# Five feed-forward blocks begun on the first token half, kept in memory, and the T3 operands made on VectorE

## The chip, the cores and the metric

The kernel runs on one core of one Trainium2 chip. A core has TensorE for matrix products, VectorE, ScalarE and GpSimd for elementwise work, queues that issue memory transfers (those of SyncE and ScalarE are used here), an on-chip memory (SBUF) and the accumulators of TensorE (PSUM). The metric is the device time of one execution in microseconds. All arithmetic is float32 or the 32-bit format of TensorE's products (fp32r).

## The reference

One layer of a hybrid decoder for 1,024 prompt tokens and 8 sample tokens that share the weights, 1,032 tokens in all, with a model width of 1,024. Three mixers (a gated short convolution, a state-space scan, a cross-attention) read one normalized input, are gated, added and merged; then comes the part that the change touches:

```
def swiglu(xn, w_gate, w_up, w_down):
    return (jax.nn.silu(xn @ w_gate) * (xn @ w_up)) @ w_down
...
xp = xp + h
xp = xp + swiglu(rmsnorm(xp, norm_ffn_w[l]), w_ffn_gate[l], w_ffn_up[l], w_ffn_down[l])
```

The hidden width is 2,816, that is 22 blocks of 128 columns. The same is done for the sample tokens, and a last normalization follows.

## The kernel before

**Layout.** Activations lie transposed: 8 tiles of 128 channels by 1,032 tokens. A float32 product is made of three fp32r products: each operand is split into a high part (a cast on ScalarE) and the rest (a subtraction on VectorE), and TensorE multiplies high by high, high by low and low by high. `st_split` does this for weights (L220), `split_to` for activations (L327).

**Stages.** The three mixers, their gates and the merge take until about 1,864 us of the span; the merge (L1522 to L1555) goes over the tokens in two halves of 516 and leaves the sums of the residual in eight tiles `x2`. Then come the gate and up products of the feed-forward part (L1568 to L1619), and then the down product and the last normalization.

**The fast matrix product.** The gate and up products are made pair by pair: pair (g, j) holds the hidden blocks j and j+1 of `w_ffn_gate`, pair (u, j) those of `w_ffn_up`, for j = 0, 2, ... 20. Weights and activations are cut into two by two blocks: the activations by the first and last four channel tiles and by the two token halves (B11 and B21 are the first token half, B12 and B22 the second), the weights by the same channel halves and the two hidden blocks. `strassen` (L271) makes the four output blocks from seven products in place of eight. Its operands on the activation side are B11, B21, B22 and four sums and differences of blocks, named T1, nT2, T3 and T4 in the code. They are the "forms": for each, four tiles of 128 x 516 are computed, cast (high) and subtracted (low), once for all 22 pairs. On the weight side, S, T and D are built for every pair from the two raw weight blocks (`st_sums`, `st_sums2`). One product (`st_prod`, L230) is 24 matmuls of 128 x 128 by 258 columns: four channel tiles, three fp32r products, two halves of columns. Products accumulate in PSUM tiles `m0`, `m1`, `m2` of two banks each.

**The order of the products.** For a plain pair: weights A times B11, S times T1, S times nT2, A times B21, T times T3, T times B22, D times T4, with evictions to the output tiles between them (ScalarE copies and VectorE adds and subtracts). For the first three pairs, (g, 0), (u, 0) and (g, 2), `st_early` (L242) makes the two products that need B11 and B21 alone, ahead of all the others. Those forms come from the first token half, whose merge and normalization are done earlier (`form_first` and `form_second`, queued in the merge's second half). The result of `st_early`, a tile of 128 x 1,032, holds A times B11 in its second half and the finished output block of the first token half in its first. It stays in a slot of the pool `ev`, and `strassen` takes it as `early` and makes only the other five products; it then reaches the second half of that tile through `S.copy(o21, o12)` (L307), `V.tensor_sub` (L308) and `V.tensor_tensor` (L309).

**The forms of the second token half.** After the last merge block, the norm of the second half is made (`norm_half`), and the forms follow in the order T1, nT2, T3, B22, T4 (L1571 to L1591), with the sums of g0's weights among them (`g0`). All are made by VectorE with ScalarE's casts, but for T3: its difference and its low part are GpSimd's (L1583, L1584).

**Slots.** The pool `ev` has 5 slots: early tiles, weight sums, `sq` and `rf` of the norm. Raw weights have 3 slots (`raw`), split weights 3 each (`whi`, `wlo`). The pool `big` has 8, which hold the eight `x2` tiles until the forms are made and the outputs of the pairs after that.

**What sets the order.** The order of instructions on each engine is fixed when the program is built: a planner goes through the program with modelled durations, and places an instruction when its inputs and slots are there by that model. Three chains keep weight loads, casts and splits in program order (`in_turn`, L110). Weight loads, reloads and the stores of the hidden blocks are issued by SyncE's queue; the stores of `x2` by ScalarE's.

Of the kernel before, what the change touches and what calls it, by code (L numbers as in the profile page):

```python
# [12 lines left out]
ALU = mybir.AluOpType  # L13
# [4 lines left out]
P = 128  # L18
# [3 lines left out]
TT = T + NS  # L22
# [19 lines left out]
def tile_kernel(ctx: ExitStack, tc, a, o):  # L42
    nc = tc.nc
    V, S, G, PE, SY = nc.vector, nc.scalar, nc.gpsimd, nc.tensor, nc.sync

    def f32(t):
        return t.bitcast(F32)
# [13 lines left out]
    def mm_ps(name):  # L61
        return pmm[0].tile([P, NCH, 512], F32, tag="mm", name=name)

    def sm_ps(name):
        return psm.tile([P, 512], F32, tag="sm", name=name)

    def dram(name, shape):
        return dp.tile(shape, F32, tag=name, name=name)

    def act_tile(part, name, dt=F32R, shape=(P, TT)):  # L70
        return ap_.tile(list(shape), dt, tag=part, name=name)
# [4 lines left out]
    def t3(t, lo=0):  # L76
# [9 lines left out]
        out=tri, in_=ones, pattern=[[1, P]], compare_op=ALU.is_ge, fill=0.0,  # L86
# [23 lines left out]
    def in_turn(key, ins):  # L110
        if key in prev:
            tc.add_manual_dep(
                ins.ins, prev[key].name,
                mybir.DependencyInfo(mybir.DependencyClass.NoSync, mybir.DependencyReason.DATA),
                reason="in_turn",
            )
        prev[key] = ins.ins
# [28 lines left out]
    def weights(src, name):  # L146
        raw = loaded.pop(name, None)
        if raw is None:
            raw = load_raw(src, name)
        hi = wp.tile([P, 1024], F32R, tag="whi", name=name + "h")  # L150
        lo = wp.tile([P, 1024], F32R, tag="wlo", name=name + "l")
        in_turn("hi", S.copy(hi, raw))
        in_turn("lo", V.tensor_sub(lo, raw, f32(hi)))
        return hi, lo

    def ev_tile(name, shape=(P, TT + 4), dt=F32):
        return ev.tile(list(shape), dt, tag="ev", name=name)
# [22 lines left out]
    def gemm(w, acts, name, width=P, off=0):  # L180

        hi, lo = w
        ps = mm_ps(name)
        nk = len(acts)
        marks = {nk * i // pace[0] for i in range(pace[0])}
        for k, (ah, al) in enumerate(acts):
            if k in marks:
                tick()
            ks = slice(k * width + off, k * width + off + P)
            for i, (wt, x) in enumerate(((hi, ah), (hi, al), (lo, ah))):  # L190
                for n in range(NCH):
                    PE.matmul(  # L192
                        ps[:, n, :CW], wt[:, ks], x[:, n * CW : (n + 1) * CW],
                        start=(k == 0 and i == 0), stop=(k == nk - 1 and i == 2),
                    )
        return ps

    def wblock(w, col):
        return w[:, col : col + P].rearrange("(k p) c -> p k c", p=P)
# [5 lines left out]
    HS = [slice(0, HT), slice(HT, TT)]  # L205
# [3 lines left out]
    def h3(t):  # L209
        return t.rearrange("p (n c) -> p n c", n=2)  # L210

    def hv(ps):
        return ps[:, :2, :HC]

    def st_raw(src, name):
        raw = wp.tile([P, 1024], F32, tag="raw", name=name)
        in_turn("raw", SY.dma_start(raw.rearrange("p (k c) -> p k c", k=KD), src))
        return raw

    def st_split(src, name, n=1024):  # L220
        hi = wp.tile([P, 1024], F32R, tag="whi", name=name + "h")
        lo = wp.tile([P, 1024], F32R, tag="wlo", name=name + "l")
        in_turn("hi", S.copy(hi[:, :n], src))
        in_turn("lo", V.tensor_sub(lo[:, :n], src, f32(hi)[:, :n]))
        return hi, lo

    def st_ps(tag, name):
        return pst[0].tile([P, 2, 512], F32, tag=tag, name=name)

    def st_prod(forms, ps, w, off, f, start):  # L230
        for kt in range(4):
            xh, xl = forms[f][kt]
            ks = slice(off + kt * P, off + (kt + 1) * P)
            for i, (wt, x) in enumerate(((w[0], xh), (w[0], xl), (w[1], xh))):
                for n in range(2):
                    PE.matmul(  # L236
                        ps[:, n, :HC], wt[:, ks], x[:, n * HC : (n + 1) * HC],
                        start=(start and kt == 0 and i == 0), stop=(kt == 3 and i == 2),
                        skip_group_check=True,
                    )  # L240

    def st_early(blocks, forms):  # L242


        held = []
        for i, (src1, nm, o1) in enumerate(blocks):
            wA = st_split(st_raw(src1, f"{nm}Er"), f"{nm}E")
            ps = st_ps(f"m{i}", f"{nm}e")
            st_prod(forms, ps, wA, 0, "B11", True)
            S.copy(h3(o1[:, HS[1]]), hv(ps))  # L250
            held.append((wA, ps, o1))
        for wA, ps, o1 in held:
            st_prod(forms, ps, wA, 512, "B21", False)
            S.copy(h3(o1[:, HS[0]]), hv(ps))

    def st_sums(src1, src2, nm, sums):
        raw1, raw2 = st_raw(src1, f"{nm}r1"), st_raw(src2, f"{nm}r2")
# [5 lines left out]
    def st_sums2(raw1, raw2, sa, nm, sums):  # L263
        sb = sums(f"{nm}sb")
        V.tensor_add(sb[:, :512], raw1[:, :512], raw2[:, :512])
        V.scalar_tensor_tensor(
            sb[:, 512:], sa[:, 512:], -1.0, raw1[:, 512:], op0=ALU.mult, op1=ALU.subtract
        )
        return st_split(sb, f"{nm}T")
# [54 lines left out]
            return o21  # L324
        return hv(pa)

    def split_to(hi, lo, src, eng=V):  # L327
        S.copy(hi, src)
        eng.tensor_tensor(lo, src, f32(hi), op=ALU.subtract)


    xT_d = dram("xT_d", [KD, P, TT])
# [7 lines left out]
    r_d = dram("r_d", [1, TT])  # L340
    x2_d = dram("x2_d", [KD, P, TT])
    h_d = dram("h_d", [NF, P, TT])
    q_d = dram("q_d", [8, P, TT])
    k_d = dram("k_d", [2, P, D])
    v_d = dram("v_d", [2, P, D])
# [23 lines left out]
    with tc.tile_pool(name="p0", bufs=1) as p0:  # L369
# [13 lines left out]
        for key, src, n in (  # L383
# [14 lines left out]
            while done < n:  # L398
                b, off = divmod(at, P)
                m = min(n - done, P - off)  # L400
# [3 lines left out]
        ps = sm_ps("ps_prm")  # L404
# [26 lines left out]
        for g3 in range(3):  # L431
# [3 lines left out]
            src = [(t, P) for t in xin[3 * g3 : 3 * g3 + 3]]  # L435
# [3 lines left out]
            for i, (t, n) in enumerate(src):  # L439
                j = 3 * g3 + i  # L440
# [10 lines left out]
            ps = sm_ps(f"ps_rb{g3}")  # L451
            blocks(ps, lambda i, t, n: bc(rst[:n, 3 * g3 + i : 3 * g3 + i + 1], [n, P]))
            V.tensor_copy(rbc[:, c], ps[:, :n_all])
            for k in range(KD):
                ps = sm_ps(f"ps_xt{g3}{k}")
# [13 lines left out]
    for src, dst, nr, nt in (  # L469
# [4 lines left out]
        for q0 in range(0, nt, per):  # L474
            t = ev_tile(f"hist{nr}_{q0}", (nr, per * P))
            SY.dma_start(t, src[:, q0 * P : (q0 + per) * P])
            ps = sm_ps(f"ps_h{nr}_{q0}")
# [23 lines left out]
    def small(name):  # L501
        return pd_.tile([P, W], F32, tag=name, name=name)

    x0, mx, u, z, z2, q = (small(n) for n in ("x0", "mx", "u", "z", "z2", "q"))
# [948 lines left out]
    def big(name):  # L1453
        return ph2.tile([P, TT], F32, tag="big", bufs=8, name=name)
# [3 lines left out]
    for m in range(KD):  # L1458
# [4 lines left out]
        ps = gemm(weights(wblock(a["w_attn_o"][0], m * P), f"wo3{m}"), acts, f"po3{m}")  # L1463
# [36 lines left out]
    def normed(m, half):  # L1500
        t = x2[m][:, HS[half]]
        V.scalar_tensor_tensor(t, t, par("ffn", m), rfs[half][:, :HT], op0=ALU.mult, op1=ALU.mult)  # L1502
        return t


    forms = {}
    fx = {}

    def form(f, kt, src, eng=V):
        if kt % 2 == 0:  # L1510
            mk = fx.get(f) or (lambda part, nm: act_tile(part, nm, shape=(P, 2, HT)))
            pair = (mk("ah", f"{f}{kt}h"), mk("al", f"{f}{kt}l"))
            forms.setdefault(f, []).extend(tuple(t[:, i, :] for t in pair) for i in range(2))
        split_to(*forms[f][kt], src, eng)

    def form_first(kt):
        form("B11", kt, normed(kt, 0))
# [4 lines left out]
    for half in range(2):  # L1522
        sq = ev_tile(f"sq{half}")
        for m in range(KD):
# [3 lines left out]
            ps = mm_ps(f"pm{half}{m}")  # L1528
# [12 lines left out]
            t = x2[m][:, HS[half]]  # L1541
# [24 lines left out]


    ffn = {"g": a["w_ffn_gate"][0], "u": a["w_ffn_up"][0]}  # L1568
    early = {(nm, j): ev_tile(f"{nm}{j}e") for nm, j in (("g", 0), ("u", 0), ("g", 2))}
    st_early([(wblock(ffn[nm], j * P), f"{nm}{j}", t[:, :TT]) for (nm, j), t in early.items()], forms)  # L1570
    for kt in range(4):  # L1571
        b12, b11 = normed(kt, 1), x2[kt][:, HS[0]]
        V.tensor_sub(b11, b12, b11)
# [3 lines left out]
    for kt in range(4):  # L1577
        t1, b22 = x2[kt][:, HS[0]], normed(kt + 4, 1)
        V.tensor_sub(t1, t1, b22)
        form("nT2", kt, t1)  # L1580
    for kt in range(4):
        b12, b22 = x2[kt][:, HS[1]], x2[kt + 4][:, HS[1]]
        G.tensor_tensor(b12, b22, b12, op=ALU.subtract)  # L1583
        form("T3", kt, b12, G)  # L1584
    g0 = (*g0, st_sums2(*g0[:3], "g0", ev_sums))
    for kt in range(4):
        form("B22", kt, x2[kt + 4][:, HS[1]])
# [5 lines left out]
    def hidden_pair(nm, j):  # L1593
        o = []
        e = early.get((nm, j))

        def outs():
            o.extend([big(f"{nm}{j}o1") if e is None else e[:, :TT], big(f"{nm}{j}o2")])
            return tuple(t[:, c] for t in o for c in HS)

        src = ffn[nm]
        pa = strassen(
            wblock(src, j * P), wblock(src, (j + 1) * P), forms, f"{nm}{j}",
            ev_sums, outs, e, ready=g0 if (nm, j) == ("g", 0) else None,
        )
        return o[0], o[1], pa if e is None else h3(pa)
# [99 lines left out]
    for n3 in range(3):  # L1706
        c0, c1 = 384 * n3, min(384 * n3 + 384, TT)
        w = c1 - c0
        for m0 in range(0, KD, 3):
            ms = range(m0, min(m0 + 3, KD))  # L1710
            ps = mm_ps(f"pl{n3}{m0}")
# [46 lines left out]
```

## Time and profile before

| what | value |
|---|---|
| median of 3 runs | 2605.4 us (2601.82 to 2606.6) |
| the profiled execution | 2603.75 us, span 2601.7 us |
| mean granted clock of TensorE | 0.988 |
| TensorE busy | 2521.7 us, 97% of the span |
| VectorE busy | 1466.5 us, 56% |
| ScalarE busy | 936.6 us, 36% |
| GpSimd busy | 197.9 us, 8% |
| memory traffic | 389.31 MB, mean 150 GB/s |

A row of a timeline has the start and the length of a group of like instructions in microseconds, the engine (PE is TensorE, PEld its weight loads, DVE is VectorE, ACT ScalarE, POOL GpSimd, SP SyncE; a q behind the name is the engine's queue), the line of the kernel, the operation, the tile written and those read, their shapes and the count; a bracket tells the idle time before and what ended it. Many instructions of the feed-forward part have the line of a helper (L236 for the matmuls of `st_prod`, L329 for the low parts of the forms, L224 for those of the weights), so they are told apart by their tiles: `g0m` is the PSUM of pair (g, 0), `g0e` that of its early block, `T10l` the low part of form T1. A row of stages has, for each engine, busy time and count, then the granted clock, the share of the DMA engines and GB/s.

### The profile page before, as it was taken

To read this page: it belongs to the slowest core of one execution; us is meant where nothing else is said; L and a number is where in the kernel's file an instruction comes from. 1 tells how busy PE (TensorE), PEld (TensorE's weight loads), DVE (VectorE), ACT (ScalarE), POOL (GpSimd) and SP (SyncE) were. 2 spreads that over 40 slices of the span, in tenths; PEclk is the share of its full clock that TensorE was granted. 3 is DMA by queue.
4 is the path that set the end of the run, shared out by engine and by line. 5 is a ranking of instruction groups with operands and counts; after the bars stand their busy time and mean duration, and the time that the engine had idled before them with its cause. 6 is when DMAs were issued, how large, how long until landed. Compare 5 with 4: busy or idle time off the path is not lost.

```text
span 2601.7 us, 42760 instructions
## 1 busy us (share of the span) xinstructions
PE 2521.7 (97%) x18037; PEld 2453.8 (94%) x18037; DVE 1466.5 (56%) x2037; ACT 936.6 (36%) x1434; POOL 197.9 (8%) x211
## 2 busy tenths in 40 slices
PE   7999999999998999999999999999989999999998
PEld 5899999999998999999999898999979999999998
DVE  5844586866667655555566633444784445454316
ACT  6643444553232235354342322213343333341202
POOL 0000000013213123023000000000010000000000
PEclk9999999999999999999999999999989999999999
DMA  6244333376556755665487757854322222265211
GB/s 190 94 138 156 124 104 106 123 206 148 154 157 138 161 185 160 176 196 150 133 292 243 273 175 252 299 173 144 122 73 82 74 90 66 82 212 163 66 41 66
DMA packets 391422, 389.31 MB, mean 150 GB/s; under 512 B 15622, under 2 KB 337782, under 8 KB 391223
## 3 DMA queue, kind: packets, MB, share of 16 engines
q1 hardware_dynamic: 372654, 335.74, 43.4%
q10 hardware_dynamic: 18577, 50.84, 5.1%
q8 instruction: 142, 2.33, 0.4%
q14 instruction: 49, 0.40, 0.0%
HBM read 280.41 MB, written 106.34 MB: 149 GB/s over the span
## 4 chain that ended last, share of the span: by engine, by line
PE 68%; DMA 5%; DVE 4%; issue 1%; ACT 1%; SPq 0%; POOL 0%; ACTq 0%; DVEq 0%; POOLq 0%
PE ps_g L192 10%; PE po L192 10%; PE pd L192 8%; PE ps_scc L192 4%; PE pm L1535 4%; PE ps_q L192 4%; PE ps_scx L192 3%; PE ps_scb L192 3%; DMA kc<-in_cache_mem_k_dram 1%; PE py L797 1%; PE pss L815 1%; PE po L789 1%; DMA r<-ac_d 1%; PE u20m L236 1%; PE g20m L236 1%
## 5 line engine op out<-in xcount | busy, mean ns | idle before, releaser
L1658 DVE TENSOR_TENSOR x<-pd,x 128x1032 f32<-128x1032 f32 x24 | 29.5, 1231 | 131.4 <-PE pd L192 131.4
L742 ACT ACTIVATE r<-r,acum 128x128 f32<-128x128 f32 x256 | 78.9, 391 | 36.2 <-DMA r<-ac_d 34.8
L1424 DVE TENSOR_TENSOR gt<-po,gt 128x1032 f32<-128x1032 f32 x24 | 29.5, 1230 | 70.4 <-PE po L192 69.1
L776 POOL TENSOR_TENSOR xdd<-xdt,decst 128x512 f32<-128x512 f32 x32 | 46.6, 1456 | 268.1 <-DVE xdt L772 268.1
L1583 POOL TENSOR_TENSOR x<-x,x 128x516 f32<-128x516 f32 x4 | 8.9, 2235 | 635.8 <-DVE x L1502 635.8
L598 DVE SCALAR_TENSOR_TENSOR ax<-u,prm,ax 128x1024 f32<-128x1024 f32 x44 | 56.4, 1281 | 0.3 <-ACT ax L595 0.3
L882 POOL TENSOR_TENSOR st<-st,xb 128x512 f32<-128x512 f32 x32 | 43.8, 1368 | 36.2 <-DVE xb L876 34.0
L769 ACT COPY bT<-bp 128x128 f32<-128x128 f32 x32 | 8.5, 264 | 105.4 <-DVE cbm L767 105.4
L770 DVE TENSOR_TENSOR r<-r,cbm 128x1024 f32<-128x1024 f32 x32 | 39.1, 1222 | 8.6 <-ACT r L743 8.0
L806 DVE SCALAR_TENSOR_TENSOR x<-x,dpar,yt 128x128 f32<-128x128 f32 x128 | 37.5, 354 | 10.1 <-ACT yt L804 9.2
L828 POOL TENSOR_TENSOR s<-s,cdec 128x512 f32<-128x512 f32 x28 | 39.1, 1398 | 46.1 <-DVE s L821 29.6
L821 DVE TENSOR_TENSOR s<-pss,s 128x512 f32<-128x512 f32 x28 | 19.3, 688 | 38.8 <-PE pss L815 38.8
L815 PE MATMUL pss<-xdd,bT 128*128 128x512 f32 x64 | 33.8, 610 | 6.6 <-ACT bT L769 6.5
L879 POOL TENSOR_TENSOR st<-st,es 128x512 f32<-128x512 f32 x32 | 36.6, 1143 | 20.3 <-DMA st<-in_state_ssm_dram 16.7
L797 PE MATMUL py<-r,xdt 128*64 128x128 f32 x512 | 35.0, 279 | 1.5 <-issue 1.5
L767 DVE TENSOR_TENSOR cbm<-bp,tri 128x128 f32<-128x128 f32 x32 | 9.3, 290 | 45.3 <-PE bp L762 45.2
L743 ACT ACTIVATE r<-r 128x1024 f32<-128x1024 f32 x32 | 33.9, 1059 | 0.7
L793 DVE TENSOR_TENSOR yt<-po,ea 128x512 f32<-128x512 f32 x28 | 19.2, 686 | 25.7 <-PE po L789 25.7
L797 PEld LDWEIGHTS py<-r,xdt 128*64 128x64 f32 x512 | 27.3, 136 | 5.8 <-issue 2.4
L1263 ACT ACTIVATE pr<-psa,mx 128x256 f32<-128x256 f32 x32 | 14.9, 472 | 48.8 <-DVE mx L1261 48.8
L1253 DVE TENSOR_TENSOR kc<-kc,qb 128x1024 f32<-128x1024 f32 x16 | 19.6, 1224 | 22.0 <-DMA kc<-in_cache_mem_k_dram 21.9
L1542 DVE TENSOR_TENSOR x<-pm,xT 128x516 f32<-128x516 f32 x16 | 11.1, 695 | 36.2 <-PE pm L1535 36.2
(7961 smaller groups left out, 8684.3 us busy)
## 6 DMA issues: line engine op xcount, KB each, us to landing
gt<-gt_d SPq DMA_DIRECT2D x32, 516.0 KB
r<-ac_d SPq DMA_DIRECT2D x32, 512.0 KB
gt_d<-g ACTq DMA_DIRECT2D x24, 516.0 KB
mg_d<-gt SPq DMA_DIRECT2D x24, 516.0 KB
mg<-mg_d SPq DMA_DIRECT2D x24, 516.0 KB
xs_d<-ax ACTq DMA_DIRECT2D x22, 516.0 KB
hr<-h_d SPq DMA_DIRECT2D x22, 516.0 KB
zs_d<-z ACTq DMA_DIRECT2D x16, 516.0 KB
```

Source lines behind the costliest of these rows:

```text
L192: PE.matmul(ps[:, n, :CW], wt[:, ks], x[:, n * CW : (n + 1) * CW], start=(k == 0 and i == 0), stop=(k == nk - 1 and i == 2),)
L236: PE.matmul(ps[:, n, :HC], wt[:, ks], x[:, n * HC : (n + 1) * HC], start=(start and kt == 0 and i == 0), stop=(kt == 3 and i == 2), skip_g ...
L598: V.scalar_tensor_tensor(acc[:, :T], u[:, j : j + T], w[j], acc[:, :T], op0=ALU.mult, op1=ALU.add)
L742: S.activation(r[:, h, :], r[:, h, :], AF.Relu, scale=-1.0, bias=acum[:, c, h0 + h : h0 + h + 1])
L770: V.tensor_tensor(r, r, bc(cbm.unsqueeze(1), [P, HPG, P]), op=ALU.mult)
L776: G.tensor_tensor(b3(xdd, HPG), b3(xdt, HPG), bc(decst[:, c, hs].unsqueeze(2), [P, HPG, 64]), op=ALU.mult)
L797: PE.matmul(py[hp : hp + 64, (h // 2) * P : (h // 2 + 1) * P], xdt[:, h * 64 : (h + 1) * 64], r[:, h, :], start=True, stop=True,)
L806: V.scalar_tensor_tensor(xg[t][:, cs], xg[t][:, cs], dpar[:, g * 4 + t : g * 4 + t + 1], yt[:, t, :], op0=ALU.mult, op1=ALU.add,)
L815: PE.matmul(pss, bT, xdd, start=True, stop=True)
L828: ins = G.tensor_tensor(b3(s_new, HPG), b3(state["s"], HPG), bc(cdec[:, c, hs].unsqueeze(2), [P, HPG, 64]), op=ALU.mult,)
L882: G.tensor_tensor(st, st, xb, op=ALU.add)
L1535: PE.matmul(ps[:, n, :HC], wt[:, ks], x[:, half * HT + n * HC : half * HT + (n + 1) * HC], start=(k == 0 and i == 0), stop=(k == KD - 1 an ...
```

## The change

Five early blocks are made in place of three, in two groups: (g, 0), (u, 0), (g, 2) first, then (u, 2) and (g, 4). The early tile of (g, 0) stays in its slot as before. Those of the other four are stored to a scratch in device memory, `e_d`, by ScalarE's queue as soon as both products are evicted; when `strassen` comes to such a pair, SyncE's queue loads the tile into the pair's first output tile, a slot of `big`. Pairs (u, 2) and (g, 4) thereby change from the plain form to the early form. And T3's difference and low part move from GpSimd to VectorE.

```
     def st_early(blocks, forms):
-        held = []
-        for i, (src1, nm, o1) in enumerate(blocks):
-            wA = st_split(st_raw(src1, f"{nm}Er"), f"{nm}E")
-            ps = st_ps(f"m{i}", f"{nm}e")
-            st_prod(forms, ps, wA, 0, "B11", True)
-            S.copy(h3(o1[:, HS[1]]), hv(ps))
-            held.append((wA, ps, o1))
-        for wA, ps, o1 in held:
-            st_prod(forms, ps, wA, 512, "B21", False)
-            S.copy(h3(o1[:, HS[0]]), hv(ps))
+        for first in range(0, len(blocks), 3):
+            held = []
+            for i, (src1, nm, out, keep) in enumerate(blocks[first : first + 3]):
+                wA = st_split(st_raw(src1, f"{nm}Er"), f"{nm}E")
+                ps = st_ps(f"m{i}", f"{nm}e")
+                o1 = out()
+                st_prod(forms, ps, wA, 0, "B11", True)
+                S.copy(h3(o1[:, HS[1]]), hv(ps))
+                held.append((wA, ps, o1, keep))
+            for wA, ps, o1, keep in held:
+                st_prod(forms, ps, wA, 512, "B21", False)
+                S.copy(h3(o1[:, HS[0]]), hv(ps))
+                keep(o1)
...
-    early = {(nm, j): ev_tile(f"{nm}{j}e") for nm, j in (("g", 0), ("u", 0), ("g", 2))}
-    st_early([(wblock(ffn[nm], j * P), f"{nm}{j}", t[:, :TT]) for (nm, j), t in early.items()], forms)
+    early = {}
+    blocks = []
+    for i, (nm, j) in enumerate((("g", 0), ("u", 0), ("g", 2), ("u", 2), ("g", 4))):
+
+        def keep(t, i=i, key=(nm, j)):
+            if i == 0:
+                early[key] = t
+            else:
+                early[key] = e_d[i - 1]
+                S.dma_start(e_d[i - 1], t)
+
+        blocks.append(
+            (wblock(ffn[nm], j * P), f"{nm}{j}", lambda nm=nm, j=j: ev_tile(f"{nm}{j}e")[:, :TT], keep)
+        )
+    st_early(blocks, forms)
...
         b12, b22 = x2[kt][:, HS[1]], x2[kt + 4][:, HS[1]]
-        G.tensor_tensor(b12, b22, b12, op=ALU.subtract)
-        form("T3", kt, b12, G)
+        V.tensor_sub(b12, b22, b12)
+        form("T3", kt, b12)
...
         def outs():
-            o.extend([big(f"{nm}{j}o1") if e is None else e[:, :TT], big(f"{nm}{j}o2")])
+            if (nm, j) == ("g", 0):
+                o.append(e)
+            else:
+                o.append(big(f"{nm}{j}o1"))
+                if e is not None:
+                    SY.dma_start(o[0], e)
+            o.append(big(f"{nm}{j}o2"))
             return tuple(t[:, c] for t in o for c in HS)
```

More of the change, by code (lines that the diff above doesn't have):

```diff
@@ L325, in strassen, with split_to @@
         return hv(pa)
-    def split_to(hi, lo, src, eng=V):
+    def split_to(hi, lo, src):
         S.copy(hi, src)
-        eng.tensor_tensor(lo, src, f32(hi), op=ALU.subtract)
+        V.tensor_sub(lo, src, f32(hi))
     xT_d = dram("xT_d", [KD, P, TT])
@@ L342, in tile_kernel @@
     h_d = dram("h_d", [NF, P, TT])
+    e_d = dram("e_d", [4, P, TT])
     q_d = dram("q_d", [8, P, TT])
@@ L1507, in tile_kernel, with form @@
     fx = {}
-    def form(f, kt, src, eng=V):
+    def form(f, kt, src):
         if kt % 2 == 0:
@@ L1513, in form @@
             forms.setdefault(f, []).extend(tuple(t[:, i, :] for t in pair) for i in range(2))
-        split_to(*forms[f][kt], src, eng)
+        split_to(*forms[f][kt], src)
     def form_first(kt):
```

## The prediction

> **What bounds the kernel now.** I read the page's head first, then the busy times by stage, then TensorE, VectorE and GpSimd in order of time through the one stage that stands out, and last the chain of waits there. A difference under 0.2% (5.2 us) is about what a measurement of this kernel can't tell from no change.
>
> ```profile
> span 2601.7 us, 42760 instructions
> ...
> 1864.80:1884.30 19.50, 19.46 (x162) 19.40 (x163) 16.09 (x26) 8.14 (x16) 3.90 (x1) 1.00 0.14 43
> 1884.30:1917.80 33.50, 21.47 (x130) 19.82 (x129) 31.05 (x37) 17.08 (x27) 11.76 (x7) 0.75 0.16 47
> 1917.80:1986.70 68.90, 68.90 (x573) 68.84 (x571) 40.38 (x54) 22.68 (x30) 0.00 (x0) 1.00 0.29 93
> ```
>
> In the stage rows the columns are busy time and count for TensorE, its weight loads, VectorE, ScalarE and GpSimd, then granted clock, DMA share and GB/s. TensorE is full and at full clock before and after 1884.3 to 1917.8, and only there it isn't: 21.47 us busy of 33.50 at a clock of 0.75. In the stage after it, 573 matmuls take 68.90 us, 0.1202 us each; at that pace the 130 of the hole take 15.6 us. So 17.9 us (0.7% of the span) is lost there, and that is all a cover for this stage can win. The timeline of TensorE says where ("x2" is a pair of matmuls; the bracket is the idle time before it and who ended it):
>
> ```profile
> 1889.87 0.51 PE L236 MATMUL g0m<-nT20l,g0Sh 128*128 128x258 f32 x2 [1.54 <-DVE nT20l L329]
> ...
> 1891.57 0.51 PE L236 MATMUL g0m<-nT22l,g0Sh 128*128 128x258 f32 x2 [0.72 <-DVE nT22l L329]
> ...
> 1893.92 0.80 PE L236 MATMUL g0m<-nT22h,g0Sh 128*128 128x258 f32 x2 [1.60 <-ACT nT22h L328]
> 1898.32 0.80 PE L236 MATMUL g0m<-nT22l,g0Sh 128*128 128x258 f32 x2 [3.60 <-DVE nT22l L329]
> ...
> 1900.34 0.80 PE L236 MATMUL g0m<-B220h,g0Th 128*128 128x258 f32 x2 [0.80 <-ACT g0o L300]
> 1900.94 0.63 PE L236 MATMUL g0m<-B220l,g0Th 128*128 128x258 f32 x2
> 1901.37 0.63 PE L236 MATMUL g0m<-B220h,g0Tl 128*128 128x258 f32 x2
> ...
> 1908.54 0.80 PE L236 MATMUL g0m<-T30h,g0Th 128*128 128x258 f32 x2 [3.71 <-DVE g0e L309]
> ```
>
> Six gaps add to 12.0 us, and the remaining 5.9 us is slow clock: pairs start 0.43 us apart (1900.94 to 1901.37) where they start 0.24 apart elsewhere. Every gap ends on a form made by VectorE or ScalarE, or on an eviction queued among those forms. VectorE, in its turn:
>
> ```profile
> 1882.64 2.46 DVE L1502 SCALAR_TENSOR_TENSOR x<-x,prm,rf 128x516 f32<-128x516 f32 x2
> ...
> 1898.18 0.68 DVE L1590 SCALAR_TENSOR_TENSOR x<-x,x 128x516 f32<-128x516 f32 x1
> ...
> 1899.40 1.21 DVE L224 TENSOR_TENSOR g0Tl<-g0sb,g0Th 128x1024 fp32r<-128x1024 f32 x1
> 1900.53 0.68 DVE L329 TENSOR_TENSOR B220l<-x,B220h 128x516 fp32r<-128x516 f32 x1
> 1901.14 1.29 DVE L329 TENSOR_TENSOR B222l<-x,B222h 128x516 fp32r<-128x516 f32 x2
> ```
>
> and GpSimd beside it:
>
> ```profile
> 1890.92 3.43 POOL L329 TENSOR_TENSOR T30l<-x,T30h 128x516 fp32r<-128x516 f32 x2
> 1894.31 3.40 POOL L329 TENSOR_TENSOR T32l<-x,T32h 128x516 fp32r<-128x516 f32 x2
> ```
>
> From 1882.64 to 1898.18 VectorE starts 11 instructions (nine of nT2, two of g0's second sum) in 15.54 us; after that a form of the same kind has its successor 0.61 us behind it (1900.53 to 1901.14). The slow stretch is the one in which GpSimd makes T3, and GpSimd's instructions come at 1.7 us each (3.43 for two) where VectorE's take 15.54 / 11 = 1.4 on the mean; it ends when GpSimd's last one does (1894.31 + 3.40 = 1897.71). The chain of waits runs over VectorE's forms up to L309 and then over TensorE to the end of T4, at 1917.8.
>
> ```profile
> 1907.80 0.69 DVE g0e L309
> ...
> 1914.69 3.14 PE g0m L236 x24
> ```
>
> **The change, part by part.** *Two more early blocks (u2, g4).* Each is 48 matmuls moved ahead of the forms: 2 x 48 x 0.1202 = 11.5 us of TensorE work, moved and not added, from stages where it is full anyway into the wait. *T3 on VectorE.* GpSimd's eight instructions become 8 x 0.61 = 4.9 us of VectorE; the 11 slowed ones go from 15.5 to 11 x 0.61 = 6.7 us, 8.8 us given back. *Two weight splits move forward:* 1.13 us each on VectorE (g0Tl, 1899.40 to 1900.53), 2.3 us. VectorE's unbroken run, which now ends with L309 at 1908.5, so ends at 1908.5 - 8.8 + 4.9 + 2.3 = 1906.9.
>
> TensorE meets that run thus: 1884.3 + 11.5 = 1895.8 is when T1 is first needed (T1's forms are made before 1882.64 already; nine instructions of nT2 and the two splits behind it take 7.8 us, to about 1890.5); then T1, nT2, B22 at 2.9 us each to 1904.5, T3 to 1907.4, T4 to 1910.3. The last forms at 1906.9 arrive about when T4 begins. Cover and run are almost equal, so I don't book the whole 17.9 us. Two leftovers: the g0 pair's T1 goes into the PSUM tile m1 that g4's early block must first leave, an eviction like that ahead of 1900.34 (0.80 us, say 0.9); and forms late by a little, for which I take 2.0 us, between 0 (the sum just made) and 9.6 (the first rival). Behind the gap of 1.54 us a pair takes 0.51 us, where the slow ones take 0.80, so I charge these gaps for themselves alone. 17.9 - 0.9 - 2.0 = 15.0 us.
>
> The Trainium skill ("TensorE: Matmul & The Clock Gate", section "What's actually happening") has the clock halve only after an idle window of about 3.4 us. By that rule leftovers of 0.9 and 2.0 us cost nothing more. The trace disagrees: the pair at 1893.92 is already slow after gaps of 1.54, 0.72 and 1.60 us with work between. By the rows a slow spell of nine pairs, 0.19 us each, could come on top, 1.7 us, and the gain would be 13.3; by the rule it is 15.0.
>
> *The way through memory.* Each stored block adds one DMA issue on ScalarE's queue behind its own eviction, and one on SP's; two weight blocks are read once more (st_sums reads again what the early block read).
>
> ```profile
> 1864.79 0.33 ACTq L1548 DMA_DIRECT2D x_d<-x  x1
> ...
> 1903.12 0.63 ACT L307 COPY u0o<-u0e 128x516 f32<-128x516 f32 x1 [1.79 <-DVE T40l L329]
> ```
>
> ```profile
> 1854.61 6.14 SPq L217 DMA_DIRECT2D g0r<-in_w_ffn_gate_dram  x2
> 1866.13 30.84 SPq L217 DMA_DIRECT2D u0r<-in_w_ffn_up_dram  x2
> ...
> 1919.35 1.70 SPq L217 DMA_DIRECT2D u2r<-in_w_ffn_up_dram  x2
> ```
>
> ```profile
> 1925.58 0.69 DVE L296 TENSOR_TENSOR u2sa<-u2r 128x512 f32<-128x512 f32 x1 [0.57 <-DMA u2r<-in_w_ffn_up_dram]
> ```
>
> Four issues of 0.33 us beside 17.08 us of ScalarE in 33.50 are hidden. The traffic, 4 x 0.516 MB out and back and 2 x 0.512 MB, 5.2 MB, falls where the DMA share is 0.14 to 0.29. A 512 KB load takes up to 4.9 us (second u2 issue at 1920.7, its reader freed at 1925.58). u0's reload needs a `big` slot, which an x2 tile leaves when T4's first form is made (L1590, 1898.18 now, near 1900 then); it lands by about 1906, and u0's L309 reads it after u0's nT2, about 1919: 13 us in hand, and the later pairs have more. If that cover goes, SP's queue holds the weights behind the reload, and ScalarE holds the T4 casts behind L307: third rival. For u2 and g4 the held form costs one ScalarE copy (0.63) and two VectorE instructions (0.68 each) more than the plain one; with VectorE at 40.38 of 68.90 us there, and u0 and g2 already of that form without a gap, that is hidden.
>
> ```profile
> 1878.35 0.40 PE L236 MATMUL g0e<-B212h,g0El 128*128 128x258 f32 x2
> ```
>
> *Weight slots.* There are three raw slots. The early loads of u2 and g4 take those that g0r's two loads have now; the second g0r load moves from about 1860.4 to when u2's split is done: the split's slot comes free with the g0e matmuls (1878.35 + 0.24), then a cast and a split, 1881.3; plus 4.9 is 1886.2. Sums and split of g0S follow by 1890; needed at 1895.8. Hidden, 6 us in hand.
>
> **The rivals.** (1) *The late g0r load stalls VectorE.* Its first reader, L259, now runs at 1876.61, between T1's forms. Order on an engine is fixed when the program is built; if L259 stays there, VectorE waits until 1886.2, 9.6 us, with the forms queued behind it.
>
> ```profile
> 1876.61 0.69 DVE L259 TENSOR_TENSOR g0sa<-g0r 128x512 f32<-128x512 f32 x1
> ```
>
> For it: VectorE has almost no slack. Against: the planner knows the slots and has forms to put ahead. 17.9 - 0.9 - 9.6, less 1.7 of slow clock, is 5.7 us: 2599.7. (2) *VectorE's slow pace belongs to the stage, not to GpSimd:* T3 then adds 8 x 1.7 = 13.6 us and the splits 2.3; g0 ends 15.9 later with 11.5 us more work done: 4.4 us slower, 2609.8. Against it: both ends of the slow stretch lie on GpSimd's. (3) *The reloads come late* (slower): ScalarE's L307 stands waiting in order, as it does for 1.79 us at 1903.12, with casts and evictions behind; or SP holds the reload behind a weights load that waits for its slot, as the second u0r did for 30 us. It decides once the four reloads together stall TensorE for over 15 us, 3.8 us each; at one full load time and a half, 7.3 us each, 29 us, the result is 14 us slower, 2619. Against: SP's order puts the loads for an earlier need first, and 13 us are in hand. (4) *The second group isn't early:* if its split, its eviction slot (five `ev` tiles, three in use, each kept until its store lands) or its PSUM tile holds it up until the forms are done, only VectorE's relief stays, 8.8 - 4.9 = 3.9 and about 1 of clock: 2600.5. Against: rf1 and sq1 leave their slots by about 1888.
>
> **How the numbers follow.** The profiled run took 2603.75 us, its span 2601.7 plus 2.0 around it; less 15.0 it is 2588.8. That run stands 1.65 below the median of 2605.4, so the median forecast is 2605.4 - 15.0 = 2590.4; the rivals' times are from the median likewise. Chances: forecast 0.76 (its own range 2587 to 2596, from 17.9 to about 9 us), rival 1 0.06, rival 2 0.03, rival 3 0.08, rival 4 0.07. The range 2585 to 2602 holds the forecast and rivals 1 and 4, less their tails. Faster: the forecast and half of rivals 1 and 4, 0.82; same: the other half and some of 2, 0.08; slower: rival 3 and the rest of 2, 0.10.
>
> **What would show it.** Right: no GpSimd work after 1870; VectorE's forms at 0.6 us throughout; ten early products to about 1896 without a gap; g0's last matmul near 1913 against 1917.8; clock near 1.00 in that stage; no TensorE gap in u0 to g4. Wrong: a VectorE wait for a weights load before T1's last form; a ScalarE wait for a reload at L307 with casts behind it; gaps in TensorE at u0, g2, u2 or g4.

## The result and the profile after

The changed kernel takes 2595.41 us (median of 8 runs, 2588.74 to 2599.30) beside 2605.74 us before (8 runs): a ratio of 0.9961, 95% interval 0.9951 to 0.9971, that is 10.3 us or 0.4% faster. Forecast were 15.0 us. Its profiled execution took 2593.12 us, with a span of 2591.4 us.

The stages of the changed kernel, in the columns of the prediction's stage rows (TensorE, weight loads, VectorE, ScalarE, GpSimd, clock, DMA share, GB/s):

```profile
1863.20:1895.00 31.80, 31.80 (x265) 31.70 (x266) 28.44 (x47) 17.00 (x30) 0.00 (x0) 1.00 0.33 109
1895.00:1913.50 18.50, 15.64 (x116) 14.96 (x115) 16.32 (x25) 11.81 (x18) 0.00 (x0) 0.91 0.47 143
1913.50:1928.00 14.50, 14.50 (x122) 14.47 (x121) 12.06 (x18) 4.57 (x6) 0.00 (x0) 1.00 0.43 135
1928.00:1946.00 18.00, 16.23 (x122) 16.02 (x121) 10.19 (x14) 5.54 (x7) 0.00 (x0) 0.91 0.48 155
1946.00:1961.60 15.60, 14.71 (x122) 14.50 (x121) 10.24 (x14) 4.61 (x7) 0.00 (x0) 1.00 0.21 69
```

The stage up to 1895, with all ten early products, is full. The hole of before is gone but for a rest in pair g0 (second row), and two smaller holes have come in pairs g2 and u2 (fourth and fifth row), where before there was none. TensorE's waits between 1895 and 1965, longest first (total, times, longest):

```profile
PE g2m L236 <- DVE g2o L312: 1.8, 1, 1.8
PE g0m L236 <- DVE g0e L312: 1.7, 1, 1.7
PE u2m L236 <- DVE u2o L312: 0.9, 1, 0.9
PE g0m L236 <- ACT u0Sh L223: 0.8, 1, 0.8
PE g0m L236 <- ACT g0o L303: 0.3, 1, 0.3
```

L312 is the line that was L309: VectorE's eviction of nT2, which frees the PSUM tile that T3 needs.

**Where to measure.** The first matmul of the feed-forward part, g0e, starts at 1864.84 us before and at 1863.18 after: 1.66 us of the difference lies ahead of anything the change touches. Over all profiled executions of this study that start lies between 1860.9 and 1868.4, while the time from g6's first matmul to the down product is 325.6 us in all of them. So I compare the stretch from g0e's first matmul to g6's first: 142.03 us before, 133.26 after, 8.77 us won. With the 1.66 at the start and 0.1 lost at the end that is the 10.3 us between the two spans. What TensorE loses in that stretch, counted as the time by which its pairs of matmuls start later than 0.24 us after each other:

| kernel | stretch, us | lost in g0 | lost elsewhere | ratio to before, interval |
|---|---|---|---|---|
| before | 142.03 | 18.2 | none | 1 |
| changed | 133.26 | 4.8 | g2 3.5, u2 1.2 | 0.9961 (0.9951 to 0.9971) |
| e1, T3 alone | 136.79 | 12.9 | none | 0.9982 (0.9974 to 0.9991) |
| e2, blocks alone | 137.63 | 3.4 | early u2 0.5, early g4 7.1, u0 0.4, g2 1.1, u2 1.2 | 0.9989 (0.9980 to 0.9998) |
| e3, three through memory | 136.75 | 12.8 | none | 0.9980 (0.9971 to 0.9989) |
| e4, sums behind L312 | 128.83 | 4.9 | none | 0.9949 (0.9936 to 0.9961) |
| e5, reloads ahead | 128.07 | 3.7 | u2 0.7 | 0.9962 (0.9949 to 0.9975) |
| e6, T4 behind L312 | 130.13 | 1.0 | u0 1.4, u2 3.8 | 0.9969 (0.9958 to 0.9980) |
| e7, e4 and a sixth block | 124.85 | none | g4 1.0 | 0.9942 (0.9929 to 0.9954) |
| e8, e4 and e6 together | 126.36 | 1.0 | u0 1.3 | 0.9946 (0.9934 to 0.9959) |

(About 2.2 us around g0e's start, which all ten share, are left out. The stretch is from one execution each. By the medians, e1 to e8 all win less than by the stretch: 0.7 to 2.4 us less, and 4.8 in e5 and 3.8 in e6. The medians also carry the scatter ahead of the stretch, but whether that is the whole reason isn't shown. The intervals of e4 to e8 overlap that of the changed kernel, so what these runs win over it rests on the stretch.)

### The profile page after: what moved, and what is told of

Its sections match the earlier page's. It is cut to its first block, busy times and chain, and to the rows that moved or that the text cites. A ratio compares the mean times of both kernels' runs of the same rounds, so it can differ in the third digit from the quotient of the medians.

```text
span 2591.4 us, 42766 instructions
## 1 busy us (share of the span) xinstructions
PE 2520.2 (97%) x18037; PEld 2453.2 (95%) x18037; DVE 1463.4 (56%) x2049; ACT 937.1 (36%) x1436; POOL 184.6 (7%) x203
## 4 chain that ended last, share of the span: by engine, by line
PE 68%; DMA 5%; DVE 4%; ACT 1%; issue 1%; POOL 0%; SPq 0%; DVEq 0%; ACTq 0%; POOLq 0%
PE po L192 11%; PE ps_g L192 9%; PE pd L192 8%; PE ps_scc L192 4%; PE pm L1539 4%; PE ps_q L192 4%; PE ps_scx L192 3%; PE ps_scb L192 3%; DMA kc<-in_cache_mem_k_dram 2%; PE py L801 1%; PE pss L819 1%; PE po L793 1%; DMA r<-ac_d 1%; PE u20m L236 1%; PE g20m L236 1%
## 5 line engine op out<-in xcount | busy, mean ns | idle before, releaser
L1428 DVE TENSOR_TENSOR gt<-po,gt 128x1032 f32<-128x1032 f32 x24 | 29.5, 1229 | 74.7 <-PE po L192 68.0
L1468 DVE TENSOR_TENSOR gt<-po,gt 128x1032 f32<-128x1032 f32 x8 | 9.9, 1232 | 38.6 <-PE po L192 38.6
```

## The experiments

**e1: T3 on VectorE, nothing else.**

```
-        G.tensor_tensor(b12, b22, b12, op=ALU.subtract)
-        form("T3", kt, b12, G)
+        V.tensor_sub(b12, b22, b12)
+        form("T3", kt, b12)
```

> Three early blocks held on the chip as before; only T3 goes to VectorE. My theory (cover and relief add up): VectorE's run loses the 8.8 us of slow pace and gains 4.9 us, so L309 ends 3.9 us sooner and some slow clock goes with it: 4 to 7 us faster, about 2600; TensorE still idle several times between 1884 and 1910. Rival (the whole gain of 10.3 us is T3's): 2595. Rival (VectorE's slow pace is not GpSimd's): 2609.

Measured: 2596.88 us beside 2601.09, a stretch 5.2 us shorter. So T3 is about half of the gain (5.2 of 8.8 us), not all, and VectorE's slow pace was GpSimd's: it is gone. The holes of before are now nearly a single one. In order of time, TensorE, then ScalarE and VectorE of e1:

```profile
1897.32 0.80 PE L236 MATMUL g0m<-B220h,g0Th 128*128 128x258 f32 x2 [9.46 <-ACT g0o L300]
```

```profile
1896.15 0.62 ACT L328 CAST T40h<-x 128x516 fp32r<-128x516 f32 x1 [2.55 <-DVE x L1590]
1896.68 0.58 ACT L300 COPY g0o<-g0m 128x516 f32<-128x516 f32 x1
```

```profile
1895.38 1.90 DVE L1590 SCALAR_TENSOR_TENSOR x<-x,x 128x516 f32<-128x516 f32 x3
```

TensorE waits 9.46 us for T1's eviction, and that stands on ScalarE behind a cast of T4 which waits for L1590, T4's differences, late in VectorE's run of forms. That is the stretch which more early blocks can cover.

**e2: five early blocks through memory, T3 left on GpSimd.** The changed kernel, with e1's edit turned back:

```
-        V.tensor_sub(b12, b22, b12)
-        form("T3", kt, b12)
+        G.tensor_tensor(b12, b22, b12, op=ALU.subtract)
+        form("T3", kt, b12, G)
```

> Five early blocks through memory; T3 stays on GpSimd. My theory: 11.5 us of cover against forms that end 2.3 us later than before; with the 4.7 us that the changed kernel loses in pairs g2 and u2 unchanged, 4 to 8 us faster, about 2599, and VectorE again at 1.4 us an instruction beside GpSimd. Rival (cover alone does it): 2594. Rival (the way through memory eats the cover): 2605 or more.

Measured: 2599.09 us beside 2601.09, a stretch 4.4 us shorter. By the stretch the parts alone give 5.2 and 4.4 us, 9.6 in sum, and both together 8.8, so they nearly add up. By the medians it is 4.2 and 2.0 us against 10.3, and 2.0 is less than the 4 to 8 that I expected. The losses are also not those that I expected: g2 and u2 lose 2.3 us in place of 4.7, and the early block g4 loses 7.1. VectorE doesn't go at 1.4 us an instruction throughout. For a while GpSimd is the one held up: two of its T3 differences take 9.51 us while VectorE keeps 0.6 us each. ScalarE then waits for GpSimd with an eviction behind it, and TensorE for that (GpSimd, VectorE, ScalarE, TensorE of e2):

```profile
1883.63 9.51 POOL L1600 TENSOR_TENSOR x<-x,x 128x516 f32<-128x516 f32 x2 [4.87 <-DVE x L1506]
```

```profile
1885.27 1.29 DVE L1607 SCALAR_TENSOR_TENSOR x<-x,x 128x516 f32<-128x516 f32 x2
1886.48 1.29 DVE L332 TENSOR_TENSOR nT22l<-x,nT22h 128x516 fp32r<-128x516 f32 x2
```

```profile
1891.95 0.62 ACT L331 CAST T32h<-x 128x516 fp32r<-128x516 f32 x1 [4.42 <-POOL x L1600]
1893.18 0.62 ACT L331 CAST T32h<-x 128x516 fp32r<-128x516 f32 x1 [0.61 <-POOL x L1600]
1893.71 0.58 ACT L252 COPY g4e<-g4e 128x516 f32<-128x516 f32 x1
```

```profile
1894.34 0.80 PE L236 MATMUL g4e<-B210h,g4Eh 128*128 128x258 f32 x2 [4.64 <-ACT g4e L252]
```

**e3: T3 on VectorE, and only the three early blocks of before, two of them through memory.**

```
-    for i, (nm, j) in enumerate((("g", 0), ("u", 0), ("g", 2), ("u", 2), ("g", 4))):
+    for i, (nm, j) in enumerate((("g", 0), ("u", 0), ("g", 2))):
```

> T3 on VectorE, and the three early blocks of before, of which u0 and g2 go through memory: against the run with T3 alone this prices the way through memory. My theory (store and reload are hidden; the losses in g2 and u2 come with a late weights load): within 1.5 us of the run with T3 alone. Rival (each reload stalls TensorE): 3 to 4 us slower than that run for two reloads, with gaps in u0 and g2.

Measured: 2597.03 us beside e1's 2596.88, the stretch 136.75 beside 136.79 us. Store and reload of two blocks cost nothing that can be seen. The rival of late reloads is out for them.

**e4: the weight sums of g4 and u4 behind L312 of g2 and u2, on VectorE.**

```
+            l12[nm] = V.tensor_tensor(h3(o12), hv(pa), h3(o12), op=ALU.add)
...
+        behind(nm, V.tensor_add(sa[:, :512], raw2[:, :512], raw2[:, 512:]))
```

`behind` is an ordering edge on VectorE alone, for g4 after g2 and for u4 after u2; no wait is added.

> The changed kernel, with one thing moved on VectorE: the first weight sum of pair g4 (and u4) may only stand behind the eviction L312 of pair g2 (and u2). My theory (VectorE stands in order before g4's late weights load, with the eviction that TensorE's T3 waits for queued behind it): the gaps of 1.8 us in g2 and 0.9 us in u2 go, and the slow clock after the first: 4 to 4.7 us faster than the changed kernel, about 2591. Rival (the reload itself is what is late): the gaps stay, 2595.

Measured: 2588.61 us; the stretch is 4.4 us shorter than in the changed kernel, and the losses in g2 and u2 are gone. In the changed kernel, VectorE stands before g4's late load, with L312 behind it:

```profile
1935.58 0.69 DVE L262 TENSOR_TENSOR g4sa<-g4r 128x512 f32<-128x512 f32 x1 [3.15 <-DMA g4r<-in_w_ffn_gate_dram]
1936.19 0.69 DVE L312 TENSOR_TENSOR g2o<-g2m,g2o 128x516 f32<-128x516 f32 x1
```

In e4, L312 (now L323) comes first, as soon as TensorE is done, and the sum (L273) waits no longer, since the load has landed meanwhile. The load took less time here (4.5 us from issue to landing, where it took 5.5), but its last part landed at 1938.89, after L323 had begun; in the old order L323 would still have waited for it:

```profile
1938.30 0.70 DVE L323 TENSOR_TENSOR g2o<-g2m,g2o 128x516 f32<-128x516 f32 x1 [1.56 <-PE g2m L236]
1938.91 0.69 DVE L273 TENSOR_TENSOR g4sa<-g4r 128x512 f32<-128x512 f32 x1
```

**e5: all four reloads issued behind pair g0.**

```
         s1, s2, pa = hidden_pair("g", j)
+        if j == 0:
+            for key in list(early)[1:]:
+                t = big(f"{key[0]}{key[1]}o1")
+                SY.dma_start(t, early[key])
+                early[key] = t
```

> The changed kernel with all four reloads issued together, right behind the g0 pair, in place of one at the head of each pair; VectorE's order as in the changed kernel. It tells why g4's second weights load lands late (5.5 us from issue to landing, against 3.9 in the kernel before). My theory (it shares the transfer engines with u2's reload and two stores of hidden blocks): it lands 1 to 1.6 us sooner, and the gap of 1.8 us in g2 shrinks to under 1, that of 0.9 in u2 likewise: 2 to 4 us less for the stage than in the changed kernel. Rival (the load's issue is late, not its transfer): the gaps stay.

Measured: 2591.64 us; a stretch of 128.07 us, 5.2 shorter than in the changed kernel. The gap in g2 is gone and that in u2 shrunk to 0.4 us. (1.1 us of the 5.2 are g0's, where the gap stayed but no slow clock followed it; what e5 changes doesn't explain that, see the last section.) But the gaps didn't shrink for the reason I gave. g4's second load takes no less time than in the changed kernel (1930.08 to 1935.58 there, 5.5 us): it is issued at 1935.36 and its reader starts at 1941.44, 6.1 us.

```profile
1934.73 0.53 SPq L1645 DMA_DIRECT2D h_d<-g0o  x1
1935.36 0.37 SPq L217 DMA_DIRECT2D g4r<-in_w_ffn_gate_dram  x1
```

```profile
1937.97 0.70 DVE L312 TENSOR_TENSOR g2o<-g2m,g2o 128x516 f32<-128x516 f32 x1 [1.56 <-PE g2m L236]
1941.44 0.69 DVE L262 TENSOR_TENSOR g4sa<-g4r 128x512 f32<-128x512 f32 x1 [1.35 <-DMA g4r<-in_w_ffn_gate_dram]
```

The planner, with other slots free at other times, happened to place L312 ahead of the sum. VectorE still waits 1.35 us for the load, and nobody waits for VectorE. So the order decides, and u2's reload isn't needed to make the load late. Crowding by other transfers isn't excluded: in place of the reload, g4's own first load is issued 1.2 us ahead of the second here. What makes a load that took 3.9 us before take 5.5 to 6.1 wasn't settled. In both slower cases two stores of hidden blocks are issued within 2.5 us of it, and before they lie 5.8 us and more ahead of it; but in e4, with the same neighbours as in the changed kernel, the load took 4.5.

**e6: the low parts of T4, and u0's weight sums, behind L312 of g0.**

```
+        if defer:
+            t4late.append(lambda: V.tensor_sub(lo, src, f32(hi)))
...
+            while t4late:
+                tc.add_manual_dep(
+                    t4late.pop(0)().ins, l12[nm].ins.name,
```

> The changed kernel with VectorE's low parts of T4 (and u0's weight sums) put behind L312 of pair g0, the eviction that TensorE waits 1.7 us for; pairs g2 and u2 as in the changed kernel. My theory (the eviction isn't slow, it stands in line behind four ready subtractions; the slow clock comes from that gap): L312 ends near 1902.3 in place of 1905.3 by the changed kernel's times, the gap and the slow spell behind it go, 3 to 4.5 us less for the stage. Rival (VectorE's run itself is the bound): the gap comes back at T4, less than 1 us won.

Measured: 2592.74 us; a stretch of 130.13 us, 3.1 shorter than in the changed kernel. g0's loss falls from 4.8 to 1.0 us: the eviction had stood in line behind ready subtractions. Some of it came back: 1.4 us in u0, whose weight sums are now late. In g2 nothing is lost any more, though no edge was set there, and in u2 3.8 us in place of 1.2, because the load that VectorE stands before for long is now u4's:

```profile
1946.04 0.69 DVE L312 TENSOR_TENSOR u4sa<-u4r 128x512 f32<-128x512 f32 x1 [3.09 <-DMA u4r<-in_w_ffn_up_dram]
1946.65 0.69 DVE L279 TENSOR_TENSOR u4sb<-u4r,u4r 128x512 f32<-128x512 f32 x1
1947.25 0.69 DVE L325 TENSOR_TENSOR u2o<-u2m,u2o 128x516 f32<-128x516 f32 x1
```

**e7: e4 with a sixth early block, (u, 4).**

```
-    e_d = dram("e_d", [4, P, TT])
+    e_d = dram("e_d", [5, P, TT])
...
-    for i, (nm, j) in enumerate((("g", 0), ("u", 0), ("g", 2), ("u", 2), ("g", 4))):
+    for i, (nm, j) in enumerate((("g", 0), ("u", 0), ("g", 2), ("u", 2), ("g", 4), ("u", 4))):
```

> The run with the sums behind L312 (e4), with a sixth early block, u4: 5.8 us more cover. My theory (cover and VectorE's run were almost equal, so 2.9 us of lateness is bought off by more cover): g0's loss falls from 4.9 us to under 1.5, 3 to 5 us faster than e4, about 2585. Rival (the wait moves along with the later start of T1, since VectorE also has a third split): g0's loss stays near 5; or a gap at u4, whose reload comes last.

Measured: 2585.01 us beside 2600.81; the stretch is 124.85 us, 4.0 shorter than e4. g0 loses nothing now: more cover hides what e6 took away by order. All that is left in the stretch is one wait:

```profile
PE g4m L236 <- DVE g4o L323: 0.8, 1, 0.8
```

By its median this is the fastest of the ten kernels (0.9942 of before, with an interval that overlaps those of e4 and e8), and its stretch is 8.4 us shorter than the changed kernel's.

**e8: both orders, e4 and e6.** The edits of both; the pairs of the edges are

```
+    after_l12 = {"u0": "g0", "g4": "g2", "u4": "u2"}
```

> Both moves on VectorE together: g4's and u4's sums behind L312 of g2 and u2, and T4's low parts behind L312 of g0. If the two losses are what I take them for, they add: the stage is 8 to 9 us shorter than in the changed kernel, 17 us shorter than before, the whole 17.9 us of the hole but about 1: about 2588 beside 2605 of before. Rival (one bound replaces the other): no better than the better of the two alone.

Measured: 2586.26 us; a stretch 6.9 us shorter than in the changed kernel and 15.7 shorter than before, where 8 to 9 and 17 were expected. The two gains nearly add (4.4 and 3.1 alone): the losses of 4.8 and 4.7 us are taken away, and 1.0 in g0 and 1.3 in u0, whose sums e6 had moved back, are left. L312 (now L325) runs ahead of T4:

```profile
1900.18 0.70 DVE L325 TENSOR_TENSOR g0e<-g0m,g0e 128x516 f32<-128x516 f32 x1
1900.79 1.30 DVE L354 TENSOR_TENSOR T40l<-x,T40h 128x516 fp32r<-128x516 f32 x2
```

## Why the prediction was right in direction and too large

- **The hole and the two halves of the change: right.** 17.9 us were read off the stage row; counted by pairs it is 18.2. Not all of the 5.9 us that I called slow clock is that: behind a gap at full clock the first two pairs start some 0.27 us late as well (1889.87 and 1890.21). e1 and e2 show that both parts are needed and nearly add up.
- **Cover and VectorE's run: right.** T1 was to be needed at 1895.8, which is 1894.1 with the start 1.66 us earlier, and the early blocks are done at 1894.2. L309 was to end at 1906.9, which is 1905.2 in the same way; it (now L312) ends at 1904.57 + 0.69 = 1905.3.

```profile
1902.15 1.30 DVE L332 TENSOR_TENSOR T42l<-x,T42h 128x516 fp32r<-128x516 f32 x2
1903.36 0.69 DVE L311 TENSOR_TENSOR g0o<-g0o,g0e 128x516 f32<-128x516 f32 x1
1903.97 0.69 DVE L224 TENSOR_TENSOR g0Dl<-g0r,g0Dh 128x512 fp32r<-128x512 f32 x1
1904.57 0.69 DVE L312 TENSOR_TENSOR g0e<-g0m,g0e 128x516 f32<-128x516 f32 x1
```

- **The hand-over of tile m1, 0.9 us: not paid.** The planner put nT2's first matmuls, on tile m0, between the early block and T1, and TensorE goes on at 1894.17 without a gap.
- **Late forms in g0, booked at 2.0 us: mis-sized.** The three waits in g0 add to 2.9 us, which is what I had booked in all (0.9 and 2.0), but that is luck: the longest, 1.74 us, isn't for a form. It is for L312, behind T4's low parts, as e6 shows. I had put the end of VectorE's run against the start of T4, but the run ends with the eviction that T3 waits for, and T3 was to start 2.4 us ahead of it by my own sum (1904.5 and 1906.9). On top of the waits came 1.9 us, and g0 lost 4.8: about 1.2 us of slow clock and 0.2 to 0.3 us behind each wait. I had charged the gaps for themselves alone. TensorE of the changed kernel:

```profile
1905.32 0.50 PE L236 MATMUL g0m<-T30h,g0Th 128*128 128x258 f32 x2 [1.74 <-DVE g0e L312]
...
1906.92 0.63 PE L236 MATMUL g0m<-T32h,g0Th 128*128 128x258 f32 x2
1907.35 0.63 PE L236 MATMUL g0m<-T32l,g0Th 128*128 128x258 f32 x2
...
1936.94 0.51 PE L236 MATMUL g2m<-T30h,g2Th 128*128 128x258 f32 x2 [1.77 <-DVE g2o L312]
...
1937.97 0.63 PE L236 MATMUL g2m<-T30h,g2Th 128*128 128x258 f32 x2
```

  One gap of 1.74 us, after work with no gap over 0.3 us since 1863, was enough, and one of 1.77 us after 25 us of full work. The Trainium skill ("TensorE: Matmul & The Clock Gate", section "What's actually happening") asks for an idle window of about 3.4 us; the runs disagree. The price by the row, 1.7 us for a slow spell, was nearer: it was about 1.2 us in g0 and 1.5 in g2. But not every such gap has a spell behind it (last section).
- **"u0 and g2 already of that form without a gap, that is hidden": the step that failed.** It was booked at nothing, by VectorE's busy share (40.38 of 68.90 us), and cost 3.5 us in g2 and 1.2 in u2. I had named the mechanism, a late weights load that stalls VectorE with an eviction behind it, as the first rival, but looked for it only at g0's load, where it didn't occur: that load's reader starts at 1888.98 without a wait. It came at g4's and u4's loads. e4 shows that the order on VectorE makes the loss: with only the order changed, the stretch is 4.4 us shorter and both losses are gone.
- **The way through memory: right.** e3 shows no cost for two blocks, and e4, with all four reloads in their places, loses nothing from u0 to g4. In the changed kernel ScalarE waits 3.2 us for u2's reload at L310, but TensorE's waits in u2 are for L312.
- The sum from the runs: 18.2 - 4.8 - 3.5 - 1.2 = 8.7 us, against 15.0 forecast; the stretch says 8.8. That the kernel came out at 10.3 is in part luck: 1.66 us were won ahead of the stretch.
- Of the signs named, GpSimd's rest, forms at 0.6 us and early products without a gap came true; a clock near 1.00 in g0's stage (0.91) and no gap in g2 and u2 did not.

## What to carry to other kernels

When work is moved to cover a wait, the cover can be sized from the trace (here to 0.1 us); what the sum missed were the new orders that the planner made elsewhere. Ahead of every eviction that TensorE waits for, look at what stands in front of it on its engine, and which of that waits for a load: by the stretch, an ordering edge there won half as much as the whole change (e4). Where cover and run are almost equal, buy one block more (e7), since a gap of under 2 us cost its length again in two places here.

## What the runs showed of the hardware that I had not expected

VectorE and GpSimd slow each other in either direction: before, VectorE's instructions went from 0.61 to as much as 1.7 us while GpSimd took 1.7 each; in e2, with the same T3 on GpSimd, VectorE kept 0.6 and GpSimd took 9.51 us for two. The Trainium skill ("SBUF — State Buffer", section "Who interferes with whom") tells of one engine holding a shared port for a whole instruction, with the order of issue deciding who is blocked; the two traces agree with it in that either can lose, and show in addition that the loser may lose several times in a row.

The clock of TensorE can drop after one gap of 1.74 us, yet the gaps of 0.9 us (u2 in the changed kernel) left it at 1.00. The length of a gap alone doesn't decide it. In e5 a gap of 1.77 us at the same place in g0 has no slow pair behind it, and neither has one of 1.89 us in e2. TensorE of e5:

```profile
1910.51 0.51 PE L236 MATMUL g0m<-T30h,g0Th 128*128 128x258 f32 x2 [1.77 <-DVE g0e L312]
1910.86 0.41 PE L236 MATMUL g0m<-T30l,g0Th 128*128 128x258 f32 x2
1911.10 0.40 PE L236 MATMUL g0m<-T30h,g0Tl 128*128 128x258 f32 x2
```

The granted clock in these traces changes in steps of 3.41 us: in the changed kernel it is 0.50 from 1906.78 to 1910.19 and from 1937.50 to 1940.91, and 1.00 between and around them. Counted by these steps, the full clock dropped in the stretch studied when TensorE had been idle for about 1.7 us or more within one step (1.74 and 1.77 us in the changed kernel, 1.74 in e4, 2.19 in e6), and at no other place. The end of a step cuts e5's gap into 1.30 and 0.47 us, and e2's into 1.64 and 0.25. The steps lie differently to g0e's start in each trace, so whether a gap of this size costs 1.2 to 1.5 us more looks like luck, and the stretches carry that luck. This is read off the traces and wasn't tested, and it isn't the whole rule: at about 214 us of most of these traces there is a step with 1.8 to 1.9 us idle behind which the clock stayed full.
